# Row tiles 0 to 3 of the first norm: 32x32 transposes on VectorE and a way through DRAM in place of TensorE transposes

## The chip, the cores and the metric

The kernel runs on one core of a Trainium2 chip. The engines of a core are TensorE (PE in the profile, its weight loads apart as PEld), VectorE (DVE), ScalarE (ACT), GpSimd (POOL) and SyncE (SP), each with an instruction stream that runs in order; they wait for each other by semaphores. DMAs are issued by SP and by POOL and run on 16 DMA engines. The metric is the device time of one execution in microseconds; the median of three runs before the change is 2026.43 us (2026.42 to 2026.71).

## What is computed

One encoder layer in float32 on x of 1024 positions by 1024 channels, with three norms in a row:

```python
h = layer_norm(ALPHA * h + 0.5 * swiglu(h, ffn1_w_gate, ffn1_w_up, ffn1_w_down), ln1_g, ln1_b)
h = layer_norm(ALPHA * h + hybrid_mixer(h, w_in, b_in, ...), ln2_g, ln2_b)
h = layer_norm(ALPHA * h + 0.5 * swiglu(h, ffn2_w_gate, ffn2_w_up, ffn2_w_down), ln3_g, ln3_b)
```

`swiglu` is a gated pair of products of width 2752 and a product back; `hybrid_mixer` projects h to queries, keys, values, Fourier channels and gates (`h @ w_in`), runs dilated attention and a Fourier branch and projects the merged result. The change lies between the first norm and the mixer's input projection: the product `h @ w_in` needs h with channels on the partitions, and the norm leaves it with positions on the partitions.

## The kernel before

**Products.** Every operand is split into a high part rounded to the fast 32-bit matmul type (made by ACT) and the rest (made by DVE), and a product is three matmuls: high x high, high x low, low x high. Large products are done by a seven-product (Strassen-like) scheme on 2x2 blocks. An `Operand` holds the four blocks a11, a12, a21, a22 of one side, each as two pages of 128 x 1024 (k = 4 slices of 128 channels by 512 positions); a page named `Ya110` is block a11, page 0, of the operand `X2` (called Y), `Ya110h` and `Ya110l` its high and low part.

**The place of the change.** The first feed-forward part ends with its down projection, which runs over seven products p in the order 1, 6, 2, 5, 3, 7, 4, each in 11 steps j of 12 matmuls. Products 3, 7 and 4 fill the PSUM banks called Za, Va and Ua; `qa73` is the operand page of product 7, step 3, and `qa410` that of product 4, step 10. After product 3 the rows of tiles 0 to 3 (128 positions each) are complete: `norm1` computes y1_0 to y1_3, `n_spill` keeps them in DRAM, and `X2.turn` turns them. After product 4 the same is done with tiles 4 to 7. Then the value products of the mixer begin: p = 1 (bank vA) takes block a11 of `X2` and the weights `wvb11`, then p = 2 takes a12 and `wvb21`. Blocks a11 and a12 come from tiles 0 to 3 alone, a21 and a22 from tiles 4 to 7.

**Turning a tile, before** (`turn`, from L430): eight transposes of 128 x 128 by TensorE into two PSUM banks (`tpY`), then each 128 x 128 piece is read from PSUM, multiplied by the norm's gain and shifted by its offset (`ln_cols`, per channel, so per partition after the turn), and written into its 128 columns of an `X2` page. ACT does this for the first four channel blocks (a11 or a21, L453), DVE for the others (L455). Then `derive` splits the pages into their parts; for a11 it does so in two pieces, tiles 0 and 1 first.

**What sets the order.** A planner (`Flow`) runs while the program is built. PE's products are jobs in a fixed order with nominal times; transposes are "floats" that go in between jobs when what they need is planned to be done. Work for DVE, ACT and POOL is taken by nominal due time, a load (`Q`) is put on SP when its nominal need less its lead is reached. The pages (46 of 128 x 1024) and PSUM banks are counted by the planner too. What comes out is one fixed list for each engine; on the chip each list runs strictly in order, and a wait at one instruction holds all that stands behind it.

The SP queue also waits, before each DMA, for the DMA eight places ahead of it, since it counts landings on eight semaphores in turn; POOL's queue does the same.

Of the kernel before, what the change touches and what calls it, by code (L numbers as in the profile page):

```python
# [13 lines left out]
OP = mybir.AluOpType  # L14
AX = mybir.AxisListType

P = 128
S0 = 1024
D = 1024
KD = 8  # L20
# [23 lines left out]
PAIRS = 11  # L44
FIRST = 3
MIDK = 36
LEADS = [0, 1, 2, 3, (0, 1), (1, 1), (2, 1), (3, 0), (4, 0), (5, 0), (3, 1), (4, 1), (5, 1)]


# [29 lines left out]
class Flow:  # L79
# [22 lines left out]
    def V(self, *a, **kw):  # L102
        return self.task("V", *a, **kw)
# [4 lines left out]
    def G(self, *a, **kw):  # L108
        return self.task("G", 0.0, *a, **kw)
# [8 lines left out]
    def Q(self, need, mb, fn, deps=(), lead=24.0, **kw):  # L118
        self.loads.append(Node("Q", mb, fn, deps, need, lead, **kw))
        return self.loads[-1]  # L120
# [166 lines left out]
class Builder:  # L287
# [7 lines left out]
    def page(self, name, dt=F32):  # L295
        return self.sb.tile([P, 1024], dt, name=name, tag="pg", bufs=NPG)
# [7 lines left out]
    def bank(self, name):  # L304
        return self.pp.tile([P, 512], F32, name=name, tag="ps", bufs=8)
# [6 lines left out]
def kernel(  # L312
# [6 lines left out]
    nc = tc.nc  # L319
    kb = Builder(ctx, tc)  # L320
    fl = Flow()
    page, half, bank = kb.page, kb.half, kb.bank
    V, S, G, Q, F, job = fl.V, fl.S, fl.G, fl.Q, fl.F, fl.job
# [3 lines left out]
    def as_k(t, kd=KD):  # L327
        return t.rearrange("p (k n) -> p k n", k=kd)
# [9 lines left out]
    ln_cols = kb.small([P, 32], "ln_cols")  # L338
# [3 lines left out]
    def pool_dma(*a, **kw):  # L342
        fl.queued(0.95 if "accum_op" in kw else 0.57, 4e-6 * math.prod(a[0].shape))
        nc.gpsimd.dma_start(*a, **kw)  # L344
# [72 lines left out]
    class Operand:  # L417


        def __init__(self, name, pages=2):  # L420
            self.name, self.pages = name, pages
            self.raw, self.part, self.node, self.got = {}, {}, {}, {}

        def cols(self, n, kind, k):
            return pick(self.part[n, k // 2], kind)[:, (k % 2) * 512:(k % 2) * 512 + 512]
# [4 lines left out]
        def turn(self, m, node, tile_of, c0, slack=4.0):  # L430

            hf, col = divmod(m, 4)
            ps = {}

            def run():
                y = tile_of()
                for q in range(2):
                    ps[q] = bank(f"tp{self.name}{m}{q}").rearrange("p (k n) -> p k n", k=4)
                    for j in range(4):
                        nc.tensor.transpose(ps[q][:, j, :], y[:, (4 * q + j) * P:(4 * q + j + 1) * P], ident)  # L440
            f = F(0.95, run, [node], 2, gives=1)
            for q in range(2):
                n = f"a{hf + 1}{q + 1}"
                for i in range(2):
                    def evac(n=n, i=i, q=q):
                        if (n, i) not in self.raw:
                            self.raw[n, i] = page(f"{self.name}{n}{i}")
                        for j in range(2 * i, 2 * i + 2):
                            k = c0 + 4 * q + j
                            dst = self.raw[n, i][:, (j % 2) * 512 + col * P:(j % 2) * 512 + (col + 1) * P]  # L450
                            g_, b_ = ln_cols[:, k:k + 1], ln_cols[:, k + 8:k + 9]
                            if q == 0:
                                nc.scalar.activation(dst, ps[q][:, j, :], AF.Identity, bias=b_, scale=g_)  # L453
                            else:
                                nc.vector.tensor_scalar(dst, ps[q][:, j, :], g_, b_, op0=OP.mult, op1=OP.add)  # L455
                    self.got.setdefault((n, i), []).append(
                        (V if q else S)(0.6, evac, [f], frees=i, pages=1 if col == 0 else 0, slack=slack + 6.0 * q))

        def derive(self, first, whole, lead, s1_at=6):

# [66 lines left out]
    def pair_run(cs, X, fresh, between=None):  # L527

        todo, late = [], None
        for i, c in enumerate(cs):  # L530
            if i == len(cs) - 1 and between:
                todo.append(None)
            if (c, 1) not in J and (c, 1) not in todo:
                todo.append((c, 1))
            if late:
                todo.append(late)
            if i == 0 and fresh:
                AHEAD.add(c)
                todo += [(c, p) for p in (5, 6, 2, 7)] + [(cs[1], 1), (c, 4), (c, 3)]
            else:  # L540
                todo += [(c, p) for p in (6, 2, 7, 5, 4)]
                late = c, 3
        for x in todo + [late]:
            if x is None:
                between()
            else:
                pair_job(x[0], X, x[1], 4 if x[0] == cs[-1] else 0)
# [61 lines left out]
    def lead_weights(c, w, need, leads, lead):  # L609

        def load(i):
            def run():
                if i == 0:
                    W[c, "lead"] = page(f"ld{nm(c)}")
                src = firsts[LEADS.index((c[1], i))] if c[0] == "a" else w[c[1], 0][:, i * 512:(i + 1) * 512]
                nc.sync.dma_start(W[c, "lead"][:, i * 512:(i + 1) * 512], src)
# [4 lines left out]
    def half_weights(c, need, at, lead):  # L621

        def load():
            W[c, "lead"] = page(f"ld{nm(c)}")
            nc.sync.dma_start(W[c, "lead"][:, L], firsts[LEADS.index((c[1], 1))])
        split(f"ld{nm(c)}", lambda: W[c, "lead"], lambda p: put(c, ("b21",), p),
# [560 lines left out]
    X1, X2, X3, X4 = Operand("X"), Operand("Y"), Operand("Z"), Operand("M")  # L1187
# [27 lines left out]
    def norm1(m, acc, sums, deps):  # L1215
        n, y = norm_tile(acc, sums, deps, f"y1_{m}", 1)
        unit[1, m] = G(lambda: pool_dma(n_spill[m], y()), [n])
        X2.turn(m, n, y, 0)

    ffn("a", X1, ffn1_gu, ffn1_tail, ffn1_down, lambda m, t: nc.sync.dma_start(t, x[m * P:(m + 1) * P, :]), norm1)  # L1220

# [81 lines left out]
    VJ, v_stored, VW, vb, VT = {}, {}, {}, {}, {}  # L1303
# [48 lines left out]
    for i, (to, x0, x1) in enumerate((("t1", "b11", "b12"), ("t3", "b12", "b22"), ("t2", "t1", "b22"),  # L1352
# [6 lines left out]
        n = Q(J[("a", 1 + i), 4], 1.15, copy, [vtn[x0]] if x0 in vtn else [], lead=0.0)  # L1359
# [9 lines left out]
    for i, (to, x0, x1) in enumerate((("t1", "b11", "b12"), ("t3", "b12", "b22"), ("t2", "t1", "b22"),  # L1369
# [11 lines left out]
        n = Q(J[("a", 5 + i), 4], 0.6, copy, [ttn[x0]] if x0 in ttn else [], lead=0.0)  # L1381
# [31 lines left out]
    for p, bk, new in VORDER:  # L1413
        n = PROD[p][1]
# [142 lines left out]
    for i, c in enumerate(pairs):  # L1557
        PC[c] = (c[0], i)
    pair_run([PC[c] for c in pairs], X2, True)
    X2.derive({"a11": VJ[1, 0], "a12": VJ[2, 0], "a21": None, "a22": VJ[4, 0]}, {p: VJ[p, 0] for p in PROD}, 30.0, 5)  # L1560
    for p in PROD:
        VJ[p, 0].after(X2.nodes(PROD[p][0]))
# [450 lines left out]
    for i, (to, x0, x1) in enumerate((("t1", "b11", "b12"), ("t3", "b12", "b22"), ("t2", "t1", "b22"),  # L2013
# [6 lines left out]
        n = Q(SUMS0AT[i][0], 1.15, copy, [wtn[x0]] if x0 in wtn else [], lead=0.0)  # L2020
# [69 lines left out]
    for r, n in enumerate(("b11", "b21", "b22", "t1", "t3", "t2", "t4")):  # L2090
        for i in range(2):
            k = 4 * r + 2 * i
# [83 lines left out]
    def fmid():  # L2176
        return ms_["z"][:, CK:CK + 4 * MIDK].rearrange("p (q k) -> p q k", k=MIDK)

# [6 lines left out]
    for gi in range(4):  # L2185
        st = {}

        def load(gi=gi, st=st):
            st["u"] = t = page(f"uc{gi}")
            nc.sync.dma_start(t, uf_d[gi])  # L2190
        q = Q(PJ[0], 0.5, load, [(uf_n[gi], 4.0)], 14.0 - gi, pages=1)
        t_, s_ = divmod(gi, 2)
        for i in range(2):
            def run(gi=gi, i=i, st=st):
                st["ps", i] = ps = bank(f"fc{gi}{i}")
                for j in range(4):
                    nc.tensor.matmul(ps[:, j * P:(j + 1) * P], st["u"][:, i * 512 + j * P:i * 512 + (j + 1) * P],
                                     chan[:, i, :], start=True, stop=True, skip_group_check=True)
# [19 lines left out]
            f = F(0.88, run, [q, (chan_ready, 10.0)], 1, gives=i)  # L2218
            n = S(0.42, hi, [f], pages=1 if s_ == 0 else 0, slack=2.0)
            fold_n.setdefault((t_, i), []).append(V(0.65, lo, [n] + [mz] * (1 - i), frees=1, slack=2.0))  # L2220

    for i in range(2):
# [5 lines left out]
        q = Q(PJ[0], 0.5, load, (), 22.0 - i, pages=1)  # L2228
# [34 lines left out]
    for t in range(2):  # L2263
        st = {}
# [31 lines left out]
        f = F(3.3, run, fold_n[t, 0] + fold_n[t, 1] + [pos_parts["n", 0], pos_parts["n", 1]], 3 - t, gives=2)  # L2296
# [7 lines left out]
    def mid_run():  # L2304
# [6 lines left out]
        for q in range(2):  # L2311
            for j in range(2):
                f = fmid()[:, 2 * q + j, :]
                for n, b in ((MIDK, ph), (4, pl)):
                    nc.tensor.matmul(ms_["p"][:n, q * 256:(q + 1) * 256], f[:, :n], b[:, q, j, :],
# [16 lines left out]
    f = F(1.25, mid_run, fold_n[0, 0] + fold_n[1, 0] + [pos_parts["n", 0]], 2)  # L2332
    n = V(0.3, mid_edges, [f], frees=1, slack=2.0)
    n = S(1.35, mid_hi, [n], slack=2.0)
# [18 lines left out]
    n = V(0.6, mid_raw, [PJ[2]], pages=1, slack=20.0)  # L2353
    n = S(1.06, mid_hi_w, [(n, 5.0)], pages=1)
# [82 lines left out]
    for c in range(8):  # L2437
        c2, cc = divmod(c, 2)
        st = {}
# [51 lines left out]
        q = gate_load(1, c, FJ[c])  # L2491
        n = S(0.62, sine, [FJ[c]], frees=int(c < 6 and c not in SINE.values()), halves=1)
        (seeds if c > 5 else sines)[c - 6 if c > 5 else c] = [None, n]
        n = V(1.8, outs, [n], frees=2, hgives=1, pages=1)
# [4 lines left out]
    for c in range(8):  # L2499
        n, merge = four_out[c]  # L2500
        n = V(1.38, merge, [n] + pj_n[c], gives=2, pages=2 if c % 2 == 0 else 0)
# [71 lines left out]
    for m in range(8):  # L2573
        n, y = norm_tile(lambda m=m: ya[m], lambda m=m: lw[m], done[m], f"y2_{m}", 2, 16.0 if m > 3 else -8.0)
# [133 lines left out]
def _layouts(inputs):  # L2708
# [15 lines left out]
    first = xt[0, 0].reshape(P, 4, 512).transpose(1, 0, 2)  # L2724
    out["firsts"] = np.stack([first[0]] * len(LEADS))
    out["firsts_w"] = out["ffn1_gu"][:FIRST, 0, :, :512].reshape(FIRST, P, 4, P).transpose(2, 1, 0, 3).reshape(4, P, FIRST * P)
# [42 lines left out]
```

## Time and profile before

| | |
|---|---|
| median of 3 runs | 2026.43 us |
| span of the profiled execution | 2024.4 us |
| PE busy | 2018.2 us, 9525 matmuls, clock 1.000 |
| DVE, ACT, POOL busy | 1385.4, 910.3, 283.9 us |
| TensorE transposes of the first norm's eight tiles (tpY) | 64, from 572.7 us to 644.2 us |
| first matmul of product 7 (Va), of product 4 (Ua), of the value products (vA) | 564.75, 598.24, 627.25 us |

The profile is one execution, its times count from the first instruction. "Busy" of PE is not PE at its peak: matmuls overlap, so the distance from one start to the next is the time that one takes in the stream, and the duration printed is longer. In the timeline a row gives the start, the duration, the engine, the line, the operation, out<-in and a count of merged instructions, and in brackets how long the engine had been idle and what ended that. "SPq" is SP issuing a DMA.

### The profile page before, as it was taken

To read this page: it belongs to the slowest core of one execution; us is meant where nothing else is said; L and a number is where in the kernel's file an instruction comes from. 1 tells how busy PE (TensorE), PEld (TensorE's weight loads), DVE (VectorE), ACT (ScalarE), POOL (GpSimd) and SP (SyncE) were. 2 spreads that over 40 slices of the span, in tenths; PEclk is the share of its full clock that TensorE was granted. 3 is DMA by queue.
4 is the path that set the end of the run, shared out by engine and by line. 5 is a ranking of instruction groups with operands and counts; after the bars stand their busy time and mean duration, and the time that the engine had idled before them with its cause. 6 is when DMAs were issued, how large, how long until landed. Compare 5 with 4: busy or idle time off the path is not lost.

```text
span 2024.4 us, 26430 instructions
## 1 busy us (share of the span) xinstructions
PE 2018.2 (100%) x9525; PEld 1693.1 (84%) x9525; DVE 1385.4 (68%) x2040; ACT 910.3 (45%) x1465; POOL 283.9 (14%) x484
## 2 busy tenths in 40 slices
PE   9999999999999999999999999999999999999998
PEld 8888888888888898888888888888888888888887
DVE  7765665576676878665666766887877666575566
ACT  7332433454464224665556444336533333355342
POOL 0233211111001132222122110000011111110000
PEclk9999999999999999999999999999999999999999
DMA  5789998899853386665355669883257877668753
GB/s 208 250 260 281 316 301 242 250 344 390 313 188 136 97 293 221 218 176 163 123 153 178 208 237 340 319 325 147 79 187 244 262 247 220 176 216 289 238 184 97
DMA packets 185795, 461.42 MB, mean 228 GB/s; under 512 B 21886, under 2 KB 62414, under 8 KB 185120
## 3 DMA queue, kind: packets, MB, share of 16 engines
q1 hardware_dynamic: 137376, 302.31, 43.1%
q0 software_dynamic: 48288, 157.42, 25.9%
q8 instruction: 75, 1.23, 0.2%
q14 instruction: 56, 0.46, 0.1%
HBM read 344.59 MB, written 185.29 MB: 262 GB/s over the span
## 4 chain that ended last, share of the span: by engine, by line
PE 100%; DVE 0%; DVEq 0%; issue 0%
PE Ab L502 14%; PE Aa L502 14%; PE Aq L502 8%; PE Db L502 6%; PE Da L502 6%; PE As L502 5%; PE Dq L502 3%; PE Xb L934 3%; PE Zb L934 3%; PE Za L934 3%; PE Xa L934 3%; PE Ds L502 2%; PE wA L2519 2%; PE pv L1867 2%; PE Va L934 1%; PE Vb L934 1%
## 5 line engine op out<-in xcount | busy, mean ns | idle before, releaser
L344 POOL DMA_DIRECT2D n_spill<-y x16 | 9.4, 586 | 304.5 <-DVE y L1134 233.7
L1824 ACT ACTIVATE p<-p,stat 128x192 f32<-128x192 f32 (+1 forms) x96 | 39.2, 409 | 28.1 <-DVE stat L1819 28.0
L344 POOL DMA_DIRECT2D hsba<-t2b x21 | 11.6, 552 | 265.2 <-DVE t2b L793 265.2
L344 POOL DMA_DIRECT2D hsaa<-t2a x21 | 12.9, 613 | 232.3 <-DVE t2a L793 227.1
L696 ACT ACTIVATE t2b<-Ab 128x512 f32<-128x512 f32 x21 | 12.6, 600 | 63.5 <-PE Ab L502 63.5
L789 DVE TENSOR_TENSOR t2b<-Db,t2b 128x512 f32<-128x512 f32 x21 | 14.5, 691 | 38.7 <-PE Db L502 38.7
L1119 ACT ACTIVATE y<-ya,ls 128x1024 f32<-128x1024 f32 x16 | 18.4, 1150 | 47.4 <-DVE ls L1114 36.8
L696 ACT ACTIVATE t2a<-Aa 128x512 f32<-128x512 f32 x21 | 12.6, 599 | 60.3 <-PE Aa L502 60.3
L789 DVE TENSOR_TENSOR t2a<-Da,t2a 128x512 f32<-128x512 f32 x21 | 14.5, 689 | 34.0 <-PE Da L502 34.0
L781 DVE TENSOR_TENSOR t3b<-Db,t3b 128x512 f32<-128x512 f32 x21 | 14.5, 691 | 22.5 <-PE Db L502 21.0
L502 PE MATMUL Da<-Xs40h,usa 128*128 128x512 f32 x84 | 29.3, 389 | 0.0
L502 PE MATMUL Da<-Xs41h,usa 128*128 128x512 f32 x84 | 29.3, 389 | 0.0
L502 PE MATMUL Db<-Zs40h,usb 128*128 128x512 f32 x84 | 29.3, 389 | 0.0
L502 PE MATMUL Db<-Zs41h,usb 128*128 128x512 f32 x84 | 29.3, 389 | 0.0
L781 DVE TENSOR_TENSOR t3a<-Da,t3a 128x512 f32<-128x512 f32 x21 | 14.5, 691 | 21.4 <-PE Da L502 20.6
L2609 POOL TENSOR_SCALAR zd<-ident,ls 128x128 f32<-128x128 f32 x1 | 0.4, 375 | 202.0 <-DVE ls L2618 202.0
L1589 DVE SCALAR_TENSOR_TENSOR oq<-Dq,b_cols,t3q 128x512 f32<-128x512 f32 x12 | 11.9, 989 | 24.5 <-PE Dq L502 24.4
L1867 PEld LDWEIGHTS pv<-pT,v 128*128 128x128 f32 x192 | 25.9, 191 | 1.7
L1867 PE MATMUL pv<-pT,v 128*128 128x128 f32 x192 | 27.2, 274 | 0.0
L696 ACT ACTIVATE t3b<-Ab 128x512 f32<-128x512 f32 x21 | 12.6, 601 | 26.0 <-PE Ab L502 25.8
L344 POOL DMA_DIRECT2D y_spill<-n x16 | 8.8, 551 | 96.1 <-DVE n L1150 96.1
L696 ACT ACTIVATE t3a<-Aa 128x512 f32<-128x512 f32 x21 | 12.5, 596 | 21.7 <-PE Aa L502 21.6
(7704 smaller groups left out, 7537.4 us busy)
## 6 DMA issues: line engine op xcount, KB each, us to landing
qa<-hsas SPq DMA_DIRECT2D x43, 256.0 KB, 5.2
qa<-tdat SPq DMA_DIRECT2D x43, 256.0 KB, 5.2
qb<-hsbs SPq DMA_DIRECT2D x43, 256.0 KB, 3.8
ga<-in_ffn_gu_dram SPq DMA_DIRECT2D x21, 512.0 KB, 8.4
ua<-in_ffn_gu_dram SPq DMA_DIRECT2D x21, 512.0 KB, 9.3
gb<-in_ffn_gu_dram SPq DMA_DIRECT2D x21, 512.0 KB, 4.5
ub<-in_ffn_gu_dram SPq DMA_DIRECT2D x21, 512.0 KB, 6.5
qb<-tdbt SPq DMA_DIRECT2D x33, 256.0 KB, 4.2
```

What stands on the lines that cost most here:

```text
L344: nc.gpsimd.dma_start(*a, **kw)
L502: nc.tensor.matmul(out, pick(w, a)[:, k * P:(k + 1) * P], self.cols(xn, b, k), start=first and k == 0 and ti == 0, stop=last and k == kt - ...
L696: nc.scalar.activation(H[c, t], B[c, "B"], AF.Copy)
L781: nc.vector.tensor_sub(H[c, "t3"], B[c, "D"], H[c, "t3"])
L789: nc.vector.tensor_sub(H[c, "t2"], B.pop((c, "D")), H[c, "t2"])
L934: nc.tensor.matmul(bank_, a, b, start=first and ti == 0, stop=last and ti == len(todo) - 1, skip_group_check=True)
L1119: nc.scalar.activation(st["y"], st["a"], AF.Square, bias=s[:, 2:3], scale=1.0, accum_out=s[:, 3:4])
L1589: stt(views(pages_[i], hf), views(b, None), bias[i], views(H.pop((c, t)), None), op0=OP.add, op1=op)
L1824: nc.scalar.activation(p3()[:, i, :], p3()[:, i, :], AF.Exp, bias=stats[h][:, k, 0:1], scale=1.0, accum_out=stats[h][:, k, 1:2])
L1867: nc.tensor.matmul(out, v, pt[:, sl * P:(sl + 1) * P], start=start, stop=stop, skip_group_check=True)
L2519: nc.tensor.matmul(B["w", bk, m], X4.cols(xn, a, k)[:, m * P:(m + 1) * P], pick(w, b), start=new and k == 0 and ti == 0, stop=k == 3 and t ...
L2609: nc.gpsimd.tensor_scalar(st["d"], ident, s()[:, 0:1], -1.0 / D, op0=OP.mult, op1=OP.mult)
```

## The change

For tiles 0 to 3 of the first norm `turn_far` takes the place of `turn`. DVE transposes the 128 x 1024 tile by independent 32 x 32 blocks into a page `tfY`; POOL stores this page into a DRAM tensor `farY` of 8 x 512 x 128 (channel block, position, column), in pieces of 128 elements. When all four tiles are stored, SP loads the four pages of a11 and a12, each by four DMAs, one for 32 partitions: a partition is put together from 32 runs of 32 elements (128 bytes). That finishes the turn. DVE then applies gain and offset in place, two halves of a page at a time, and `derive` splits the pages; a11 is now split as a whole, no longer in two pieces. Tiles 4 to 7 are turned as before, and so are the tiles of the second norm.

```diff
+FAR = range(4)
+FAR_LEAD = 40.0
...
+        def turn_far(self, m, node, tile_of, c0, slack=4.0):
+
+            hf, st = m // 4, {}
+            if hf not in self.far:
+                self.far[hf] = kb.dram([KD, 512, P], f"far{self.name}{hf}"), []
+            td, stored = self.far[hf]
+
+            def run():
+                st["t"] = page(f"tf{self.name}{m}")
+                nc.vector.transpose(st["t"], tile_of())
+            n = V(1.15, run, [node], pages=1, slack=slack)
+            n = G(lambda: pool_dma(td[:, (m % 4) * P:(m % 4 + 1) * P, :].rearrange("k p c -> p k c"), as_k(st["t"])), [n])
+            fl.later(n, 5.0, gives=2)
+            stored.append((n, 5.0))
+
+        def far_loads(self, hf, c0, need, lead):
+
+            td, stored = self.far[hf]
+            for q in range(2):
+                for i in range(2):
+                    n = f"a{hf + 1}{q + 1}"
+
+                    def load(n=n, i=i, q=q):
+                        self.raw[n, i] = t = page(f"{self.name}{n}{i}")
+                        for b in range(4):
+                            src = bass.AP(tensor=td.tensor, offset=td.offset + (4 * q + 2 * i) * 512 * P + 32 * b,
+                                          ap=[[P, 32], [32 * P, 32], [1, 32]])
+                            nc.sync.dma_start(t[32 * b:32 * b + 32].rearrange("p (m c) -> p m c", c=32), src)
+
+                    def scaled(n=n, i=i, q=q):
+                        for j in range(2):
+                            k = c0 + 4 * q + 2 * i + j
+                            t = self.raw[n, i][:, j * 512:(j + 1) * 512]
+                            nc.vector.tensor_scalar(t, t, ln_cols[:, k:k + 1], ln_cols[:, k + 8:k + 9], op0=OP.mult, op1=OP.add)
+                    self.got[n, i] = [V(0.75, scaled, [Q(need[q], 0.5, load, stored, lead, pages=1)], slack=4.0)]
...
     def norm1(m, acc, sums, deps):
         n, y = norm_tile(acc, sums, deps, f"y1_{m}", 1)
         unit[1, m] = G(lambda: pool_dma(n_spill[m], y()), [n])
-        X2.turn(m, n, y, 0)
+        (X2.turn_far if m in FAR else X2.turn)(m, n, y, 0)
...
     pair_run([PC[c] for c in pairs], X2, True)
+    for hf in X2.far:
+        X2.far_loads(hf, 0, [VJ[1, 0], VJ[2, 0]], FAR_LEAD)
```

The order of the instructions changes at three places; elsewhere each engine's list is the same. SP, before the change, from the last operand page of product 4 (qa with 64 rows) to the first weights of the value products:

```order
L921 DMA qa_5044<-hsaa_140 64x512
L922 DMA qa_5044<-hsaa_140 64x512
L921 DMA qa_5044<-tdat_196 64x512
L922 DMA qa_5044<-tdat_196 64x512
L1393 DMA wvb_5185<-in_in_values_dram 128x1024
L1393 DMA wvb_5187<-in_in_values_dram 128x1024
```

The same place of SP in the changed kernel (Ya_5018, Ya_5039, Ya_5093 and Ya_5098 are the pages Ya110, Ya111, Ya120 and Ya121):

```order
L959 DMA qa_5013<-tdat_196 64x512
L960 DMA qa_5013<-tdat_196 64x512
L488 DMA Ya_5018<-farY_198 32x32x32 x4
L488 DMA Ya_5039<-farY_198 32x32x32 x4
L488 DMA Ya_5093<-farY_198 32x32x32 x4
L488 DMA Ya_5098<-farY_198 32x32x32 x4
L1431 DMA wvb_5148<-in_in_values_dram 128x1024
L1431 DMA wvb_5150<-in_in_values_dram 128x1024
```

The 16 far loads stand ahead of the weights of the value products; the first of them waits for all four stores.

DVE before, the stretch that ends with the first value product's operands:

```order
L369 TENSOR_TENSOR Ya120l<-Ya_4970,Ya120h 128x1024
L369 TENSOR_TENSOR Ya121l<-Ya_4976,Ya121h 128x1024
L1061 SCALAR_TENSOR_TENSOR ya_4349<-ya_4349,p1a_4030 128x512
L1061 SCALAR_TENSOR_TENSOR ya_4351<-ya_4351,p1a_4032 128x512
L1061 SCALAR_TENSOR_TENSOR ya_4353<-ya_4353,p1a_4039 128x512
L1061 SCALAR_TENSOR_TENSOR ya_4355<-ya_4355,p1a_4041 128x512
L369 TENSOR_TENSOR wvb110l<-wvb_5185,wvb110h 128x1024
L369 TENSOR_TENSOR wvb111l<-wvb_5187,wvb111h 128x1024
L398 TENSOR_TENSOR Ya110l<-Ya_4961,Ya110h 128x2x256
```

The same stretch of DVE in the changed kernel:

```order
L494 TENSOR_SCALAR Ya_5039<-Ya_5039,ln_cols 128x512 x2
L494 TENSOR_SCALAR Ya_5093<-Ya_5093,ln_cols 128x512 x2
L494 TENSOR_SCALAR Ya_5098<-Ya_5098,ln_cols 128x512 x2
L371 TENSOR_TENSOR Ya111l<-Ya_5039,Ya111h 128x1024
L371 TENSOR_TENSOR Ya120l<-Ya_5093,Ya120h 128x1024
L371 TENSOR_TENSOR Ya121l<-Ya_5098,Ya121h 128x1024
L1099 SCALAR_TENSOR_TENSOR ya_4350<-ya_4350,p1a_4031 128x512
L1099 SCALAR_TENSOR_TENSOR ya_4352<-ya_4352,p1a_4033 128x512
L1099 SCALAR_TENSOR_TENSOR ya_4354<-ya_4354,p1a_4040 128x512
L1099 SCALAR_TENSOR_TENSOR ya_4356<-ya_4356,p1a_4042 128x512
L371 TENSOR_TENSOR wvb110l<-wvb_5148,wvb110h 128x1024
L371 TENSOR_TENSOR wvb111l<-wvb_5150,wvb111h 128x1024
```

The scaling of the pages Ya111, Ya120 and Ya121, each of which waits for its four loads, now stands ahead of the low parts of the weights wvb110 and wvb111. The scaling of Ya110 stands further ahead, before the reads of Va (p1a) and the split of qa410. On ACT the high parts follow in the order Ya110, Ya111, Ya120, Ya121, wvb110, wvb111.

On PE the 32 transposes are gone, in two groups: 16 between steps 2 and 3 of product 7 and 16 between steps 3 and 4. PE before, at the first group (tpY_4926 and the others are the PSUM banks of the transposes):

```order
L934 MATMUL Va_4840<-qa72l,qa72h 128x512
L934 MATMUL Va_4840<-qa72h,qa72l 128x512
L440 MATMUL tpY_4926<-ident,y_0_4857 128x128 x4
L440 MATMUL tpY_4931<-ident,y_0_4857 128x128 x4
L440 MATMUL tpY_4936<-ident,y_1_4883 128x128 x4
L440 MATMUL tpY_4941<-ident,y_1_4883 128x128 x4
L934 MATMUL Va_4837<-qa73h 128x512
```

In the changed kernel the two steps follow each other with nothing between them. DVE's four transposes stand where the reads of tpY were, after y_3, with the split of qa42 ahead of the fourth; the four stores stand on POOL right behind the n_spill stores of tiles 0 to 3 and ahead of two loads of `vb`, the value bias.

2 lines of the change are left out of this document (1 added, 1 removed).

## The prediction

> **What bounds the kernel now.** I read the busy shares and the chain that ended last, then the waits of TensorE (PE), then the timeline around the place of the change.
>
> ```profile
> PE 2018.2 (100%) x9525; PEld 1693.1 (84%) x9525; DVE 1385.4 (68%) x2040; ACT 910.3 (45%) x1465; POOL 283.9 (14%) x484
> PE 100%; DVE 0%; DVEq 0%; issue 0%
> PE zr L2612 <- POOL zd L2609: 1.4, 1, 1.4
> PE warm L2668 <- DVE one L331: 0.9, 1, 0.9
> ```
>
> The first line is the busy list, the second the chain, the last two all that PE waited for: 2.3 us, at the two ends of the program. So PE's instruction stream is the bound from end to end. A PE instruction taken out shortens the run by its own time if nothing new makes PE wait; a new wait lengthens it in full. The profiled execution's span is 2024.4 us, and the timed runs' median of 2026.43 lies 2.0 above it; I take that distance as unchanged.
>
> **What the change removes.** The timeline of PE around the 32 transposes (start, duration):
>
> ```profile
> 572.92 1.91 PE L440 MATMUL tpY<-ident,y 128*128 128x128 f32 x16
> 577.44 1.91 PE L440 MATMUL tpY<-ident,y 128*128 128x128 f32 x16
> 581.92 0.39 PE L934 MATMUL Va<-qa75h 128*128 128x512 f32 x1
> 584.64 0.39 PE L934 MATMUL Va<-qa76h 128*128 128x512 f32 x1
> ```
>
> From qa75 to qa76, a step of 12 products undisturbed, is 2.72 us. From 572.92 to 577.44 there are 16 transposes and one such step, 4.52 us, and from 577.44 to 581.92 again, 4.48. So the transposes hold PE for 1.80 + 1.76 = **3.56 us**, the slow restart of the next products included. The duration of 1.91 is not the price, since matmuls overlap. In the order of the instructions PE's list is otherwise the same. 3.56 us is 0.18% of the run; about 0.2% (4.05 us) is what a measurement of this kernel can tell from no change.
>
> **What it adds, and where.** The rows that time the new path, first VectorE (DVE), then POOL and SP:
>
> ```profile
> 574.09 0.82 DVE L1134 TENSOR_SCALAR y<-ya,lnrs,ls 128x1024 f32<-128x1024 f32 x1
> 574.81 2.64 DVE L455 TENSOR_SCALAR Ya<-tpY,ln_cols 128x128 f32<-128x128 f32 x8
> 582.21 1.22 DVE L369 TENSOR_TENSOR qa44l<-qa,qa44h 128x1024 fp32r<-128x1024 f32 x1
> 583.34 1.22 DVE L369 TENSOR_TENSOR qa45l<-qa,qa45h 128x1024 fp32r<-128x1024 f32 x1
> 596.40 2.73 DVE L1053 TENSOR_TENSOR p1a<-Va,p1a 128x512 f32<-128x512 f32 x4 [5.40 <-PE Va L934]
> 603.77 2.49 DVE L1061 SCALAR_TENSOR_TENSOR ya<-ya,p1a 128x512 f32<-128x512 f32 x4
> 575.20 0.53 POOL L344 DMA_DIRECT2D n_spill<-y  x1 [1.01 <-DVE y L1134]
> L344 POOL DMA_DIRECT2D comb_t<-stat x1: 1262/1262/1262, 875.2 to 875.2; - x1
> DMA to landing us min/median/max: 7.1/7.1/7.1
> 574.97 0.32 SPq L919 DMA_DIRECT2D qa<-hsaa  x1
> 578.10 0.61 SPq L922 DMA_DIRECT2D qa<-tdat  x1
> n_spill<-y POOLq DMA_DIRECT2D x16, 512.0 KB, 3.5
> v<-v_spill SPq DMA_DIRECT2D x4, 512.0 KB, 4.2
> qab<-hsba SPq DMA_DIRECT2D x32, 64.0 KB, 2.0
> ```
>
> *Transposes on DVE.* The trace has no 32x32 transpose. Of the rows with 1024 elements in a partition the cheapest takes 0.82 us and the dearest (eight pieces, 2.64 us) 2.64; I take the plain two-operand pass, 1.14 from one start to the next (582.21 to 583.34), since a transpose also reads and writes each element once. Four make 4.6 us and replace 5.3 us of reads of tpY (two groups of 2.64). They start at 574.81; with qa42l between them the fourth ends at 580.5. At 2.64 each it would end 6 us later.
>
> *Stores by POOL.* Each has 1024 pieces (128 rows of 8 blocks). A store of 128 pieces holds POOL for 0.53 us; the 1024-piece gather comb_t, 1.26. I take 1.26, so the four stores, queued behind each other, are issued by 581.8. Landing: 3.5 us for the same bytes in whole rows, plus the 0.73 of longer issue, is 584.7; with the same again for smaller pieces and n_spill beside them I put the last at **586**. The two vb loads queued behind them on POOL are used at 632 or later (the row at 635.97 below, less 3.56) and lose nothing.
>
> *Loads by SP.* SP is free at 578.7 today. In the new program the qa49 load ahead waits for PE's qa74 step (ends 581.92 - 3.56 = 578.4), which costs nothing, since PE uses its data at 619.2 (the row at 622.72 below, less 3.56). Then the first far load waits for all four stores, so 16 loads start at 586, and the wvb and wvt loads are queued behind them. Each load has 32 x 32 = 1024 pieces of 128 bytes, 64 for each of 16 DMA engines; in all 1024 pieces an engine.
>
> The price of a piece decides the change. Two windows, each with its totals and the hardware queue's line (packets, MB, share of 16 engines): 3 us in which 512-byte pieces run alone, and 16 us of mostly 2 KB pieces:
>
> ```profile
> DMA packets 1473, 0.76 MB, mean 252 GB/s; under 512 B 56, under 2 KB 1453, under 8 KB 1473
> q1 hardware_dynamic: 1473, 0.76, 89.1%
> DMA packets 1682, 3.07 MB, mean 192 GB/s; under 512 B 195, under 2 KB 195, under 8 KB 1680
> q1 hardware_dynamic: 1680, 3.04, 55.1%
> ```
>
> A 512-byte piece takes 0.891 x 16 x 3 us / 1473 = 29.0 ns. The other window (0.551 x 16 x 16 us / 1680) gives 84 ns at 1810 bytes on average. A line through both, drawn down to 128 bytes, gives 12.5 ns; no saving below 512 bytes gives 29. The row nearest in kind is the 512-byte one, the line is only drawn out, so I take the middle, **21 ns**: 1024 x 21 = 21.5 us. With 2.0 us for the latency (the shortest landing above), the last load lands at E = 586 + 2 + 21.5 = **609.5** (600.8 at 12.5 ns, 617.7 at 29). SP's issue, about 0.6 us a DMA by the row at 578.10, is 9.6 us for 16 and stays under that. Far above lies the 1024-piece gather: 7.1 us less 1.26 of issue less 2.0 is 3.8 us for 64 pieces an engine, 60 ns, with other traffic beside it: E = 649.
>
> [...]
>
> *The deadline.* What PE wants next, and when, and what stands before it on DVE and ScalarE (ACT):
>
> ```profile
> 622.72 0.39 PE L934 MATMUL Ua<-qa49h 128*128 128x512 f32 x1
> 625.44 0.39 PE L934 MATMUL Ua<-qa410h 128*128 128x512 f32 x1
> 627.25 0.39 PE L1316 MATMUL vA<-wvb110h,Ya110h 128*128 128x512 f32 x1
> 627.48 0.39 PE L1316 MATMUL vA<-wvb110l,Ya110h 128*128 128x512 f32 x1
> 590.28 1.06 ACT L364 ACTIVATE wvb110h<-wvb 128x1024 fp32r<-128x1024 f32 x1 [0.71 <-PE Va L934]
> 606.18 1.22 DVE L369 TENSOR_TENSOR wvb110l<-wvb,wvb110h 128x1024 fp32r<-128x1024 f32 x1
> 626.09 0.69 DVE L1065 SCALAR_TENSOR_TENSOR ya<-Ua,ya 128x512 f32<-128x512 f32 x1 [15.15 <-PE Ua L934]
> 635.97 1.27 DVE L1433 TENSOR_TENSOR vt<-vA,vb 128x512 f32<-128x512 f32 x2
> ```
>
> Today wvb110l is ready 20 us early. In the new order it stands on DVE behind everything made from the four pages: the scaling of Ya121, which waits for the last load (two halves, 0.8), Ya111l, Ya120l, Ya121l (3 x 1.14), four ya passes (2.5), then itself (1.2): 7.9 us behind E. The second vA product is due at 627.48 - 3.56 = 623.9, so E may be **616.0**. I forecast 609.5: 6.5 us to spare. wvb110 itself is issued when the ninth far load has landed and comes right behind the sixteenth; at 4.2 us for 512 KB plus 1.1 for its ACT half it is there by E + 5.3, before its turn at E + 6.7.
>
> Earlier on DVE, the first scaling (four loads, 586 + 2 + 5.4 = 593.4) stands ahead of p1a, qa410h and qa410l. p1a waits for PE until 592.8 anyway, and qa410 follows p1a by 2.7 + 2.5 us and is used at 621.9. Hidden. The ya passes on Ua are due at 622.5 and DVE is free at E + 9 = 618.5. Hidden too.
>
> Sum: -3.56 and no wait: span 2020.8, median **2022.9**.
>
> **Rivals.**
> 1. *The short pieces hold back the first value product* (slower). Past 27.3 ns a piece ((616.0 - 588) / 1024) each further ns costs PE 1.02 us; from 30.8 ns the gain is gone, from 34.8 ns the loss passes 0.2%. At 44 ns, half way from the 29 ns row to the gather's 60, E = 633, PE waits 17 us: 2040. For it: the price at 128 bytes is drawn out from larger pieces, and nothing else is left between the last load and PE's first product. Against: the 512-byte pieces already run at 29 ns. [...]
> 2. *The chain ahead of the loads is late.* Transposes at 2.64 us (the reads of tpY) put the stores 6 us later: E = 615.5, still in time; with 29 ns as well E = 623.7 and a wait of 7.7: 2030.6. With only part of both, a wait of 1 to 3 us: about 2025.
> 3. *The gain is taken back elsewhere*: 2026.4, if a later stage ran by DMA and not by PE. Against: PE waited for nothing between the two ends.
> 4. *More than the gain*: under 2022.4 would need a saving beyond the two groups; I see none.
>
> **How the numbers follow.** Forecast 0.58 (2022.5 to 2023.5). Rival 1 at 2026.4 or more 0.21, of which 0.17 beyond +0.2%; rivals 1 and 2 with part of the gain left 0.13; rival 3 0.04; rival 4 0.04. Faster than 2022.4: 0.06, the forecast's own edge included. Slower than 2030.5: 0.17. Within: 0.77. The range of 8 in 10 reaches from just under the full gain up to 2031, a price of 35 ns.
>
> **What would show it.** Right: DVE transposes near 1.2 us; far stores near 1.3 us on POOL; the last far load landing between 601 and 616; vA's first product near 623.7 with no PE wait for DVE or ACT; the span 3.5 us shorter. Wrong: a PE wait at the first vA products on wvb110l or wvb111l (rival 1 where the loads take over 28 us, rival 2 where they start after 590), or 3.5 us that reappear as waits further down.

## The result, and the profile after

The changed kernel takes 2023.06 us in the median (2022.64 to 2023.61), the kernel before 2026.55 beside it (2025.83 to 2026.88): a ratio of 0.9983, 95% interval 0.9977 to 0.9989. That is 3.5 us less, 0.17%. The interval lies clear of 1, so the gain is shown, although it is just under the 0.2% that the prediction took for what can be told from no change. The profiled execution has a span of 2021.2 us (2024.4 before).

The busy list and the chain of the page after, and all that PE waited for:

```profile
PE 2014.8 (100%) x9493; PEld 1689.4 (84%) x9493; DVE 1388.2 (69%) x2034; ACT 903.6 (45%) x1447; POOL 286.9 (14%) x488
PE 100%; DVE 0%; DVEq 0%; issue 0%
PE zr L2652 <- POOL zd L2649: 1.4, 1, 1.4
PE warm L2708 <- DVE one L333: 0.9, 1, 0.9
```

PE has 32 matmuls fewer (9525 before) and still waits only at the two ends of the program. Its timeline where the transposes stood, and where the value products begin:

```profile
573.13 0.39 PE L972 MATMUL Va<-qa73h 128*128 128x512 f32 x1
...
575.85 0.39 PE L972 MATMUL Va<-qa74h 128*128 128x512 f32 x1
...
578.57 0.39 PE L972 MATMUL Va<-qa75h 128*128 128x512 f32 x1
...
623.91 0.39 PE L1354 MATMUL vA<-wvb110h,Ya110h 128*128 128x512 f32 x1
624.13 0.39 PE L1354 MATMUL vA<-wvb110l,Ya110h 128*128 128x512 f32 x1
```

Two undisturbed steps of 2.72 us stand where 4.52 and 4.48 stood. The first value product starts at 623.91, before at 627.25: 3.34 us earlier, and not the full 3.56, because product 7 began 0.22 us later in this execution (564.97 for 564.75).

The new path, in the timelines of DVE, POOL and SP (the last two rows of DVE are the operand that PE needs first and the idle time behind it), and a window of the stores:

```profile
575.03 3.49 DVE L470 STREAM_TRANSPOSE tfY<-y 128x1024 f32<-128x1024 f32 x3
...
579.54 1.23 DVE L470 STREAM_TRANSPOSE tfY<-y 128x1024 f32<-128x1024 f32 x1
...
593.37 1.00 DVE L494 TENSOR_SCALAR Ya<-Ya,ln_cols 128x512 f32<-128x512 f32 x2 [4.68 <-DMA Ya<-farY]
...
602.26 2.82 DVE L494 TENSOR_SCALAR Ya<-Ya,ln_cols 128x512 f32<-128x512 f32 x6
...
610.82 1.22 DVE L371 TENSOR_TENSOR wvb110l<-wvb,wvb110h 128x1024 fp32r<-128x1024 f32 x1
...
622.75 0.69 DVE L1103 SCALAR_TENSOR_TENSOR ya<-Ua,ya 128x512 f32<-128x512 f32 x1 [9.58 <-PE Ua L972]
```

```profile
576.56 0.92 POOL L346 DMA_DIRECT2D farY<-tfY  x1 [0.62 <-DVE tfY L470]
...
581.41 0.90 POOL L346 DMA_DIRECT2D farY<-tfY  x1 [1.59 <-DVE tfY L470]
```

```profile
588.56 12.95 SPq L488 DMA_DIRECT2D Ya<-farY  x16
601.56 2.25 SPq L1431 DMA_DIRECT2D wvb<-in_in_values_dram  x4
```

```profile
582.00:589.00 7.00, 7.00 (x32) 5.79 (x31) 6.69 (x6) 1.25 (x2) 1.41 (x3) 1.00 0.98 347
```

The transposes end at 580.8, the last store is issued at 582.3, its landing at 588.5 lets SP's first load go at 588.56; in between the DMA engines are busy 98% of the time (the last row, a window: its length, busy time of each engine, granted clock, DMA share, GB/s). When the bulk of the loads ends is read from the DMA view of the window from 590 to 602 us (40 slices of 0.3 us; the totals; the hardware queue's packets, MB and share of 16 engines):

```profile
GB/s 195 181 191 153 147 189 170 163 150 178 188 178 186 140 173 180 163 181 155 175 198 167 169 188 143 197 167 187 170 134 151 165 229 167 179 186 125 21 14 14
DMA packets 15119, 1.92 MB, mean 160 GB/s; under 512 B 15118, under 2 KB 15118, under 8 KB 15118
...
q1 hardware_dynamic: 15118, 1.91, 100.9%
```

The bulk of the traffic stops after slice 37, at 601.1; the last load, issued at 599.46, lands 3.9 us later, at 603.4. A piece of 128 bytes took 1.009 x 16 x 12 us / 15118 = 12.8 ns. `wvb110l`, the last thing the second value product needs, is ready at 612.0, 12.1 us ahead of it.

### The profile page after: what moved, and what is told of

It reads as the page before. It is cut to its first block, busy times and chain, and to the rows that moved or that the text cites. A ratio compares the mean times of both kernels' runs of the same rounds, so it can differ in the third digit from the quotient of the medians.

```text
span 2021.2 us, 26394 instructions
## 1 busy us (share of the span) xinstructions
PE 2014.8 (100%) x9493; PEld 1689.4 (84%) x9493; DVE 1388.2 (69%) x2034; ACT 903.6 (45%) x1447; POOL 286.9 (14%) x488
## 4 chain that ended last, share of the span: by engine, by line
PE 100%; DVE 0%; DVEq 0%; issue 0%
PE Ab L540 14%; PE Aa L540 14%; PE Aq L540 8%; PE Db L540 6%; PE Da L540 6%; PE As L540 5%; PE Dq L540 3%; PE Za L972 3%; PE Zb L972 3%; PE Xb L972 3%; PE Xa L972 3%; PE Ds L540 2%; PE wA L2559 2%; PE pv L1907 2%; PE Vb L972 1%; PE Yb L972 1%
## 5 line engine op out<-in xcount | busy, mean ns | idle before, releaser
L346 POOL DMA_DIRECT2D hsaa<-t2a x21 | 12.8, 611 | 235.8 <-DVE t2a L831 229.6
L734 ACT ACTIVATE t2b<-Ab 128x512 f32<-128x512 f32 x21 | 12.6, 600 | 63.8 <-PE Ab L540 63.8
L734 ACT ACTIVATE t2a<-Aa 128x512 f32<-128x512 f32 x21 | 12.6, 600 | 61.7 <-PE Aa L540 61.7
L1629 DVE SCALAR_TENSOR_TENSOR oq<-Dq,b_cols,t3q 128x512 f32<-128x512 f32 x12 | 11.9, 988 | 24.5 <-PE Dq L540 24.4
L734 ACT ACTIVATE t3b<-Ab 128x512 f32<-128x512 f32 x21 | 12.6, 600 | 26.1 <-PE Ab L540 25.8
L734 ACT ACTIVATE t3a<-Aa 128x512 f32<-128x512 f32 x21 | 12.5, 597 | 21.2 <-PE Aa L540 21.1
```

Of the source, the lines that this page charges most:

```text
L734: nc.scalar.activation(H[c, t], B[c, "B"], AF.Copy)
L1629: stt(views(pages_[i], hf), views(b, None), bias[i], views(H.pop((c, t)), None), op0=OP.add, op1=op)
```

## The experiments

My theory: the gain is PE's own time for the transposes and nothing else, and the way through DRAM is hidden as long as its last load lands by 616.0. The rivals: the gain has another source (less work on DVE and ScalarE, another order), the path eats part of it, or the deadline lies elsewhere.

**The transposes back on PE, their results unused.** The path stays; beside it PE does the 32 transposes again:

```diff
+            def again():
+                y = tile_of()
+                for q in range(2):
+                    b = bank(f"again{m}{q}").rearrange("p (k n) -> p k n", k=4)
+                    for j in range(4):
+                        nc.tensor.transpose(b[:, j, :], y[:, (4 * q + j) * P:(4 * q + j + 1) * P], ident)
+            F(0.95, again, [node], 2, frees=2)
```

> The changed kernel with the 32 TensorE transposes put back beside the new path, in the same two places of PE's order (24 after qa72, 8 after qa73), their results read by nobody. Theory (the whole gain is PE's own time for the transposes, and the path through DRAM is wholly covered): 2026.6 us, the time of before (2023.1 + 3.5), with no new wait of PE. Rival (the gain comes from the reads of tpY that DVE and ScalarE no longer do, or from another order of work): it stays near 2023.1.

2026.53 us (2026.04 to 2026.87), ratio to before 1.0001 (0.9992 to 1.0010). Its timeline of PE has the transposes again, 24 ahead of step 3 of product 7 and 8 ahead of step 4:

```profile
573.42 2.78 PE L478 MATMUL again<-ident,y 128*128 128x128 f32 x24
...
578.82 1.03 PE L478 MATMUL again<-ident,y 128*128 128x128 f32 x8
```

The whole gain is gone, with no new wait, although DVE and ScalarE still read no `tpY` for these tiles. So the gain is PE's time, and the relief of the other two is worth nothing.

**The path taken away.** No transposes on DVE, no stores, four plain loads in place of 16. This kernel leaves the turning of tiles 0 to 3 out, so what follows works on unturned data:

```diff
-                            nc.sync.dma_start(t[32 * b:32 * b + 32].rearrange("p (m c) -> p m c", c=32), src)
+                        nc.sync.dma_start(t, n_spill[2 * q + i])
...
-                    self.got[n, i] = [V(0.75, scaled, [Q(need[q], 0.5, load, stored, lead, pages=1)], slack=4.0)]
+                    self.got[n, i] = [V(0.75, scaled, [Q(need[q], 0.5, load, [(unit[1, 2 * q + i], 5.0)], lead, pages=1)], slack=4.0)]
...
-        (X2.turn_far if m in FAR else X2.turn)(m, n, y, 0)
+        if m in FAR:
+            X2.far[m // 4] = None, None
+            fl.later(unit[1, m], 5.0, gives=1)
+        else:
+            X2.turn(m, n, y, 0)
```

> The changed kernel without the path: no transposes on DVE, no stores of them, and the four pages of Ya filled by four loads of 512 KB in whole rows from the stored tiles n_spill, ahead of the wvb loads as now. It leaves the turning of row tiles 0 to 3 out, so what follows works on unturned data; the arithmetic after it is the same in kind and number. Theory (the path is covered, so taking it away gives nothing): 2023.1 us, within 0.4; the last page lands before 596 in place of about 602, and the only effect is more idle time on DVE ahead of the Ua passes. Rival (the path still costs PE some of the gain, or contention with its 16384 short pieces slows something): 2022.5 or less.

2022.97 us (2022.57 to 2023.51), ratio 0.9983 (0.9974 to 0.9992), the change's own. The two rows of this kernel's DVE that answer to the last two of DVE above:

```profile
607.54 1.23 DVE L371 TENSOR_TENSOR wvb110l<-wvb,wvb110h 128x1024 fp32r<-128x1024 f32 x1
...
623.00 0.69 DVE L1100 SCALAR_TENSOR_TENSOR ya<-Ua,ya 128x512 f32<-128x512 f32 x1 [13.11 <-PE Ua L969]
```

Without the path the operand is ready 3.3 us earlier, and DVE then idles 3.5 us longer ahead of the Ua pass (13.11 for 9.58). The path costs nothing that can be measured.

**The deadline: the loads twice, two and a half times, three times.**

```diff
-                        for b in range(4):
+                        for b in [*range(4)] * 2:
```

(with `[0, 1, 2, 3, 0, 1, 2, 3, 0, 1]` and `[*range(4)] * 3` for the other two)

> The changed kernel with each of the 16 far loads issued twice (32 loads, 2048 pieces of 128 bytes for each DMA engine). In the profile of the change they took 588.6 to about 601.9, 13.3 us. Theory (deadline for the last landing E = 616.0, set by 8 us of DVE work behind it ahead of the second vA product at 624.1): E = 615.2, no wait or one under 1 us: 2023.1 to 2024. Rival (the deadline lies earlier, because the wvb loads queued behind on SP and their splits on ScalarE come later than DVE's own chain): a wait of 2 us or more at the first vA products: 2025 to 2029.

> The same with each far load issued three times: E = 588.6 + 3 x 13.3 = 628.5. Theory (deadline 616.0, beyond it every us of lateness costs PE one us): a wait of 12.5 us at the first vA products, on wvb110l, 2035.6 us (2033 to 2038). Rival (something else bounds the stage and there is more room than 616): below 2030. Rival (the wvb loads and their splits add to the chain): 2039 or more.

> The changed kernel with 40 far loads in place of 16 (each page's four loads two and a half times over). In the runs with 32 and 48 loads a load took 0.76 us, and the last one landed about 0.8 us behind the end of the issues, so E = 588.9 + 40 x 0.76 + 0.8 = 620.1, and PE's wait at the first vA products comes to about 4 us. In the run with 48 loads PE waited 11.6 us there and lost 14.2 us: its granted clock was 0.5 from about 5 us into the wait to 643. Theory (a short wait costs its own length, the clock falls only after about 5 us of it): 2023.1 + 4 = 2027 us (2026 to 2028), clock 1.0 through the stage. Rival (any wait of a few us lowers the clock behind it): 2029 to 2030.5.

Twice: 2023.17 us (2022.67 to 2024.00), ratio 0.9985 (0.9976 to 0.9994), nothing lost. Two and a half times: 2030.70 (2029.61 to 2033.53), ratio 1.0020 (1.0011 to 1.0030). Three times: 2037.27 (2036.49 to 2038.79), ratio 1.0053 (1.0037 to 1.0068). With twice the loads, the rows of DVE that start with the last page:

```profile
615.71 1.01 DVE L494 TENSOR_SCALAR Ya<-Ya,ln_cols 128x512 f32<-128x512 f32 x2 [5.13 <-DMA Ya<-farY]
...
622.44 1.22 DVE L371 TENSOR_TENSOR wvb110l<-wvb,wvb110h 128x1024 fp32r<-128x1024 f32 x1
```

The landing at 615.7 lets the chain run to 623.66, 7.95 us, and in this execution the second value product starts at 624.47: no wait, 0.8 us to spare. With two and a half times, the waits of PE, then the scaling of the last page and the second value product, then the windows of the stage (length, busy times, and the granted clock as the number ahead of the DMA share):

```profile
PE vA L1354 <- DVE wvb110l L371: 4.1, 1, 4.1
PE vA L1354 <- ACT wvb110h L366: 3.2, 1, 3.2
```

```profile
624.11 1.00 DVE L494 TENSOR_SCALAR Ya<-Ya,ln_cols 128x512 f32<-128x512 f32 x2 [7.15 <-DMA Ya<-farY]
...
632.11 0.80 PE L1354 MATMUL vA<-wvb110l,Ya110h 128*128 128x512 f32 x1 [4.07 <-DVE wvb110l L371]
```

```profile
626.00:628.00 2.00, 0.75 (x1) 0.29 (x1) 2.00 (x3) 2.00 (x3) 0.00 (x0) 0.76 1.03 422
628.00:630.00 2.00, 0.04 (x1) 0.00 (x0) 2.00 (x4) 1.90 (x3) 0.00 (x0) 0.50 1.02 418
...
631.00:635.00 4.00, 2.89 (x7) 2.31 (x8) 4.00 (x9) 0.00 (x0) 0.00 (x0) 0.50 0.65 220
635.00:639.00 4.00, 4.00 (x15) 3.16 (x14) 3.93 (x13) 3.08 (x7) 0.00 (x0) 0.72 0.11 35
```

The page lands at 624.1, 8.1 us behind the deadline, and the second product starts at 632.1, 8.0 us late: the deadline holds, and past it every microsecond of a late landing is one of a late product. (The first product waits too, 3.2 us for ScalarE's `wvb110h`, but the wait of the second ends last.) But the span grew by 10.5 us. The rest is the clock: it fell to 0.50 during the wait and came back at 637.2 (0.72 on average from 635 to 639), so PE worked for 5.1 us at half rate and lost another 2.6. This profiled execution (2033.53) is the longest of the ten, which lost 6.6 to 10.5 us; how late the pages of the others landed, no trace shows. My 2027 missed twice. The landing came 4.0 us later than I had put it (the loads began 0.6 us later, took 0.79 us each in place of 0.76, and the last was there 3.1 us behind the end of the issues in place of 0.8, which I had misread: in the runs with 32 and 48 loads it was 2.4 and 3.6); and my theory that a short wait leaves the clock alone fell. With three times the loads it is the same in the profiled execution, again the longest (2038.79): the second product 12.3 us late, half rate for 6.1 us behind it; and the median is 2037.27 where I had 2035.6, which had no clock in it.

**What a short piece costs.** Pieces of 64 bytes, and the loads shared by two issuing engines:

```diff
+                            for c in range(2):
-                                          ap=[[P, 32], [32 * P, 32], [1, 32]])
+                                              ap=[[P, 32], [32 * P, 32], [1, 16]])
-                            nc.sync.dma_start(t[32 * b:32 * b + 32].rearrange("p (m c) -> p m c", c=32), src)
+                                nc.sync.dma_start(t[32 * b:32 * b + 32].rearrange("p (m c) -> p m c", c=32)[:, :, 16 * c:16 * c + 16], src)
```

```diff
-                            nc.sync.dma_start(t[32 * b:32 * b + 32].rearrange("p (m c) -> p m c", c=32), src)
+                            (nc.sync, nc.scalar)[b % 2].dma_start(t[32 * b:32 * b + 32].rearrange("p (m c) -> p m c", c=32), src)
```

> The changed kernel with pieces of 64 bytes: 32 far loads of 1024 pieces, each covering half the bytes of one before, 2048 pieces for each DMA engine and the same bytes in all. A piece of 128 bytes took 12.8 ns by the profile of the change. Theory (the price falls in a straight line from 29.0 ns at 512 bytes through 12.8 at 128): 10.1 ns at 64, 20.7 us of loads, E about 610. Rival (a floor per piece, or the issue of 0.76 us per load with 1024 pieces): 24.4 to 26.2 us, E about 614 to 615. [...] By the first two the time stays at 2023.

> The changed kernel with the far loads of each page issued half by SP and half by ScalarE, which is idle from 583 to 594 in the profile of the change. A load of 1024 pieces took 0.76 to 0.81 us from issue to issue with 128-byte pieces, 0.72 with 64-byte pieces. Theory (the issuing engine's queue sets that price, since half the bytes hardly changed it): the 16 loads take about half as long, 6.5 to 8 us in place of 13, and the last lands by about 597. Rival (the 16 DMA engines are the bound, their busy share is 1.0 while the loads run): E stays near 602. The time is 2023 by both, since the loads are covered.

2022.89 and 2023.10 us, one execution each: hidden, as theory and rival said, for the 64 bytes and for the two queues. The DMA views, first 64 bytes in the window from 590 to 600.9, then the change in the same window, then two queues from 591 to 600 (q10 is ScalarE's):

```profile
DMA packets 15395, 0.99 MB, mean 91 GB/s; under 512 B 15394, under 2 KB 15394, under 8 KB 15394
...
q1 hardware_dynamic: 15394, 0.97, 93.2%
```

```profile
DMA packets 14839, 1.89 MB, mean 173 GB/s; under 512 B 14838, under 2 KB 14838, under 8 KB 14838
...
q1 hardware_dynamic: 14838, 1.87, 108.9%
```

```profile
DMA packets 14785, 1.88 MB, mean 209 GB/s; under 512 B 14784, under 2 KB 14784, under 8 KB 14784
...
q10 hardware_dynamic: 8297, 1.05, 74.4%
q1 hardware_dynamic: 6487, 0.82, 58.2%
```

By the prediction's formula a 64-byte piece takes 10.6 ns, near the straight line (10.1). But an engine got one only every 10.9 x 16 / 15394 = 11.3 ns, so the 32 loads took 23.1 us to issue, nearly as with twice the loads of 128 bytes (24.4), and the last landed at 614.2, where the floor had 614 to 615 and the line 610. With 128 bytes an engine finished a piece every 11.8 ns from one queue and every 9.7 ns from two, with shares of 108.9% and 132.6% (74.4 + 58.2), so the times of pieces overlap. So half the bytes hardly helped, as the floor said. A second queue took a sixth off the time of a piece and not half, and its last load landed at 602.6, which is the rival's 602 and not the theory's 597: 13.0 us behind the first issue, 14.8 with one queue, although ScalarE had two splits of its own between its loads. At 64 and 128 bytes the price goes by the piece and hardly by the byte.

**Tiles 4 to 7 by the same path, without enough other work to cover it and with it.** The bank vE belongs to value product 4, the first that takes `Ya220`, and wvt4 are its weights; `vt` is the sum that DVE makes of a bank of vA and the bias; Yrs, Ys10 and Ys11 are sums made from a21 and a22 for the products behind (vD). First the table alone (`FAR = range(8)`, a22 loaded ahead of a21); then also the eight wA products, which need tiles 0 to 3 only, ahead of vE; then also two settings of the planner:

```diff
-FAR = range(4)
+FAR = range(8)
...
     for p, bk, new in VORDER:
-        value_job(p, bk, new)
-        if p == 4:
+        if p != 4:
+            value_job(p, bk, new)
+        if p == 2:
             for p_ in (1, 2):
                 for m in range(4):
                     third_job(p_, m, p_ == 1, 2 if m == 3 else 0)
+            value_job(4, "E", True)
...
-        (X2.turn_far if m in FAR else X2.turn)(m, n, y, 0)
+        (X2.turn_far if m in FAR else X2.turn)(m, n, y, 0, 4.0 if m < 4 else 8.0)
...
-            value_part(n, i, (vblk if n in vblk else vt)[n][i], [vtn[n]] if n in vtn else (), VJ[p, 0], 14.0)
+            value_part(n, i, (vblk if n in vblk else vt)[n][i], [vtn[n]] if n in vtn else (), VJ[p, 0], 24.0 if p == 4 else 14.0)
...
```

> The changed kernel with row tiles 4 to 7 turned by the new path too (a22 loaded ahead of a21). PE loses another 32 transposes, 3.6 us. Theory (the path takes some 20 us from the last transpose to the last landing, and hides only where PE has that much other work): the tiles end at 633, the stores land at about 643, the eight loads of a22 at about 651, and Ya220 is scaled and split by 653.5 to 655, while the vE products want it at 645.7. PE waits 8 to 9 us there on Ya220h or Ya220l, more with a fall of the clock behind it: 2023.1 - 3.6 + 8.5 = 2028 (2027 to 2031). Rival (the second half hides too): 2019.5.

> As the run with both halves, and PE's eight wA products of the third value group (11.5 us of work on tiles 0 to 3 only) put ahead of the vE products, so that Ya220 is wanted at 657.2 in place of 645.7. Theory (the cover decides): Ya220 is there at 655, vE does not wait, and the gain is doubled: 2019.5 us (2019.2 to 2021). Rival (Yrs and Ys10, made from a21 and a22, or the wvt loads queued on SP behind the far loads are now late for vD at 668): a wait of 1 to 6 us, 2021 to 2026.

2031.42 us (2030.06 to 2032.19), ratio 1.0023 (1.0013 to 1.0032), and 2024.56 (2022.54 to 2025.37), ratio 0.9989 (0.9980 to 0.9998). The new waits of PE, in the first and in the second of them:

```profile
PE vA L1354 <- DVE vt L1471: 3.0, 1, 3.0
PE vE L1354 <- ACT Ya220h L366: 2.8, 1, 2.8
```

```profile
PE vA L1354 <- DVE vt L1473: 3.0, 1, 3.0
```

The wait on `Ya220h` is the one expected from too little cover, and with the later vE it is gone. It was put at 8 to 9 us and is 2.8, since PE came to vE 6.6 us later than I had put it (652.3 for 645.7), held up mostly by the other wait and its clock. That other wait I had not seen. DVE of the second kernel, and its windows:

```profile
632.46 4.61 DVE L470 STREAM_TRANSPOSE tfY<-y 128x1024 f32<-128x1024 f32 x4
636.99 2.44 DVE L1473 TENSOR_TENSOR vt<-vA,vb 128x512 f32<-128x512 f32 x4
```

```profile
636.00:637.00 1.00, 0.00 (x0) 0.00 (x0) 1.00 (x2) 0.00 (x0) 0.91 (x2) 0.92 0.87 332
637.00:638.00 1.00, 0.21 (x1) 0.24 (x2) 1.00 (x3) 0.00 (x0) 0.14 (x1) 0.50 0.97 332
...
642.00:644.00 2.00, 2.00 (x6) 1.56 (x6) 0.72 (x2) 0.00 (x0) 0.00 (x0) 0.58 0.10 35
644.00:646.00 2.00, 2.00 (x10) 1.65 (x9) 1.10 (x1) 0.00 (x0) 0.56 (x1) 1.00 0.96 160
```

The second value products add into the banks that `vt` must have read before, and `vt` stood on DVE behind the four transposes. While PE turned the tiles itself, 24 of its own transposes came ahead of the second products (in the trace of the change, 632.07 to 633.73 and 636.59 to 637.38). In the wait of 3.0 us the clock fell to 0.50, and the products ran at that rate until 643.7, 5.9 us: 2.9 more. 3.0 + 2.9 is what this kernel lacks: a span of 2023.4 for 2021.2 - 3.6 = 2017.6. Not every execution seems to pay both: the eleven took 2022.54 to 2025.37, and the two shortest, with a span of 2020.8 and a mean clock of 1.000, lack 3.2 us, about the wait alone. No trace shows these two.

> As the run with both halves and the later vE. There the only wait of PE was 3.0 us at the second vA products, for the sum vt of the first, which stood on DVE behind the four new transposes (4.6 us); the granted clock was 0.5 behind it for 5.5 us, which is another 2.7 us. Here the planner is told to let the transposes of tiles 4 to 7 wait (slack 8 in place of 4), so that two vt stand ahead of them, and to split wvt4 earlier (lead 24 in place of 14). Theory (that queue place was the whole loss): no wait, the full second gain, 2019.5 us (2019.2 to 2020.5). Rival (with the wait gone, vE comes 5.7 us earlier, at 657.3, and Ya220l or Ya221l, or Ys10 behind vE, is late for it): a wait of 1 to 3 us, and with 3 us the clock again: 2020.5 to 2025.

> The control for the last version: the changed kernel (tiles 4 to 7 still turned by PE) with only its two other edits, the wA products ahead of the vE products and wvt4 split earlier. Theory (the second gain is PE's time for the other 32 transposes, and the order only gives the cover for it): 2023.1 us, within 0.4 of the change. Rival (the new order is worth something by itself): 2019.5 to 2022.

With two `vt` ahead of the transposes and wvt4 split earlier: **2019.17 us** (2018.71 to 2019.52), ratio to before 0.9965 (0.9951 to 0.9978), 7.3 us less than before. The new order alone, tiles 4 to 7 turned by PE: 2023.03 (2022.71 to 2023.34), ratio 0.9983 (0.9974 to 0.9992), worth nothing by itself. So the second gain too is put down to PE's time; to give PE these 32 transposes back beside the path, as was done with the first 32, was not run. DVE and PE of the last version:

```profile
632.37 1.27 DVE L1473 TENSOR_TENSOR vt<-vA,vb 128x512 f32<-128x512 f32 x2
633.56 4.61 DVE L470 STREAM_TRANSPOSE tfY<-y 128x1024 f32<-128x1024 f32 x4
...
653.66 1.22 DVE L371 TENSOR_TENSOR Ya220l<-Ya,Ya220h 128x1024 fp32r<-128x1024 f32 x1
...
668.34 1.22 DVE L371 TENSOR_TENSOR Ys11l<-Yrs,Ys11h 128x1024 fp32r<-128x1024 f32 x1
```

```profile
657.39 0.39 PE L1354 MATMUL vE<-wvt40h,Ya220l 128*128 128x512 f32 x1
...
669.65 0.47 PE L1354 MATMUL vD<-wvt11h,Ys11l 128*128 128x512 f32 x1
```

`Ya220l` ends 2.5 us ahead of its product, `Ys11l`, at 669.56, only 0.1 us ahead of its own. This version has no room left.

## Why the prediction was right

- **What PE saves.** Predicted 3.56 us, measured 3.5 by the medians, and the runs that give PE the transposes back (2026.53) and take the path away (2022.97) put all of it there.
- **DVE.** 1.14 us for a transpose taken from the plain pass; three took 3.49 us, the fourth ended at 580.8 for 580.5.
- **POOL and the landing.** A store was put at 1.26 us of issue and is 0.9; the landing was put at 586 and came at 588.5, 6.2 us behind the issue of the last store. The term was mis-sized by 2.5 us: I had allowed 4.2 us, from n_spill's 3.5 and a little more, and left out that the operand pages of product 4 and the vb loads were in the queues too: the engines were busy 98% of that time. That these delayed the stores is argued; no run took them away.
- **The price of a piece.** I chose 21 ns, the middle of 12.5 and 29, and the trace says 12.8: the line through the two windows was right and my caution was not. E, the last landing, came at 603.4 in place of 609.5; the sum with the measured start and the lower price, 588.5 + 2.0 + 12.8, gives 603.3. Mechanism right, size off by 40%, in the direction that costs nothing. That the line hit is in part luck: SP's issue, put at 0.6 us a DMA and under the price of the pieces, took 0.81 us, 12.95 for the 16, as long as the pieces themselves, and two queues brought an engine a piece every 9.7 ns. So 12.8 ns is not shown to be the engine's own price.
- **The deadline.** 616.0, and 7.9 us of DVE work behind the last landing: measured 7.95, no wait at 615.7, 8.0 us of lateness for a landing at 624.1. It was the best founded number of the prediction, and the one on which most hung. The last landing had 12.6 us of room where I had 6.5.
- **Rival 1** fell with the price. It needed more than 27.3 ns a piece, and the traces say 12.8 ns at 128 bytes and 10.6 at 64, both loads from DRAM; from the first load's issue to the end of the bulk of the traffic it was 12.5 us. The price put on this rival was wrong in another way: "each further ns costs PE 1.02 us" leaves out the clock, which added 2.6 to 3.2 us to such waits in the traces. By that, an estimate, it would have been about 2043 at 44 ns, not 2040.
- **Rival 2** fell with 1.15 us a transpose: the loads did start late, by 2.5 us, but for the landing of the stores, and inside the room. The transposes' place on DVE came back as a cost for tiles 4 to 7, where they held `vt`. **Rival 3** and **rival 4** fell: nothing was taken back further down, and nothing beyond the two groups was gained.

## What to carry to other kernels

Where one engine's stream is the bound, an edit was worth that engine's time here and nothing else, so the question is only whether the new path is done before its deadline: find the deadline by walking back from the first use through everything queued behind the landing, and test it by doubling the slow step. A path of some 28 us (575.0 to 603.4) hides where the bound engine has that much other work that does not need the result; where it has less, move such work in between, and look at what the new instructions stand in front of on their own queue. A stall of PE of 3.0 us cost 5.9 in the traced execution of the later vE, 2.9 of it by the clock.

## What the runs showed of the hardware

**A short wait of PE can cost twice.** In five places of the profiled executions PE stood for 2.8 us or more: for 3.0 and 2.8 us with both halves, for 3.0 with the later vE, and with two and a half and three times the loads for 3.2 + 4.1 and 7.5 + 4.1 us, with one product between the two waits. The granted clock fell to 0.50 each time, and products stood 0.43 us apart in place of 0.23. In four of the five the windows date the fall, between 2.1 and 4.8 us after PE had stopped; in the fifth, the wait of 3.0 us with both halves, the first product behind it is already a slow one (0.77 us for 0.39). The clock was full again only 5.1 to 6.4 us after PE had set out again: 2.6 to 3.2 us lost besides the wait. The two executions of 2020.8 us above, with a mean clock of 1.000 beside a wait that was 3.0 us in the profiled one, say that the clock need not fall each time; that is argued from their times alone. What sets when it falls and when it returns is not shown.

**Pieces of 128 and of 64 bytes cost by the piece.** 12.8 ns at 128 bytes and 10.6 at 64, where 512 bytes took 29.0 in the trace before. One queue kept an engine at a piece every 11.8 ns with 128 bytes and every 11.3 with 64, two queues at one every 9.7 with 128.

What sets the limit of one queue, the issue or the engine, stays open.
